# The first stage rebuilt: x normed first, modulation as columns in two halves, projections in pairs, the chunk inverse cut in two

## The chip, the core and the metric

The kernel runs on one core of a Trainium2 chip. The metric is the device time of one execution in microseconds (us). The engines are PE (TensorE, matrix products; PEld is its weight load), DVE (VectorE), ACT (ScalarE), POOL (GpSimd) and SP (SyncE, which here only issues DMAs). SBUF is the working memory, PSUM holds the matrix products.

## What is computed

Two transformer blocks on 512 tokens of width 1024, all in float32. The change lies in the first stage of the first block:

```python
mod = silu(c) @ ada_w + ada_b          # 1024 x 6144
shift1, scale1, gate1, shift2, scale2, gate2 = split(mod, 6)
h = rms_norm(x, norm1_g) * (1 + scale1) + shift1
z = h @ w_in                            # 1024 x 3328
# columns of z: r, k, v (512 each), decay and iclr lora (64 + 64),
# gate lora (128), then q, k, v of the attention (512 each)
```

r, k, v and the lora columns are mixed with the token before (token shift) and feed a recurrence, state = state * w - (state kk)(kk a) + v k, in 8 heads. The kernel computes the recurrence in 8 chunks of 64 tokens, and for each chunk and head it needs the inverse of a 64x64 triangular matrix. The other q, k, v feed a stick-breaking attention with 8 heads. Both results go through w_out; then come a mixture of 32 experts, and a second block with convolution, sparse attention and a feed-forward part.

## The kernel before, in words

`phase_a` (L291) is the first stage. Every large product is three PE products of a high and a low part (`mm3`, L98): a weight tile is cut by `wsplit` (L112) into wh, a cast on ACT (L104), and wl = w - wh, a subtraction on DVE (L105). `wload` (L107) fetches raw weights through SP into `nraw` = 4 buffers of 512 KB.

The order at the start: `params` (L170) fetches small parameters and turns silu(c) into columns; then the 16 loads of `ada_group(0)` (L269) bring shift1 and scale1, each used at once as four one-row PE products (tile adap). x is loaded as one 2 MB transfer held back behind the seventh of these loads (L327). From adap the row tile mod is copied, turned (L332) and split into scale and shift columns (L333, L335). x is normed (L338), turned block by block (L342), and from PSUM written as hH (ACT) and as hL (DVE, L345 and L346).

Then `proj` (L366) takes 128 columns of w_in at a time: 24 products of 512 columns (8 blocks of k times 3), and before each it draws two steps of the remaining modulation, `ada_group(1)` and `(2)`, whose 32 loads feed the same kind of one-row products. First come the two lora chunks, k and r of head pair 0; the lora products follow; then, for each head pair, k, r, v and `prep` (L417), which computes Q1 and Q2 (decayed r, kk, v; and a*kk, k).

`chunk_inverse` (L635) makes XA with 64 small products (tr<-Q,Q), sends its diagonal blocks through DRAM by POOL's DMA queue (xd, XD), runs a recursion of 31 steps with two DVE instructions each (L671, L673), and sends the result back (ed, ET). Its second part turns a block (L681) and joins the two diagonal blocks by 128 products in eight groups, with a DVE copy behind each (L688, L694). The attention's q, k, v projections stand behind it in the program. The chain over chunks and the attention (`sb_heads`, L697) begin when all of this is done.

The order of instructions on each engine is chosen by a scheduler that works from estimated durations, by program order as priority. At run time every engine works its queue in that order.

Of the kernel before, what the change touches and what calls it, by code (L numbers as in the profile page):

```python
# [7 lines left out]
F32 = mybir.dt.float32  # L8
# [4 lines left out]
AF = mybir.ActivationFunctionType  # L13
OP = mybir.AluOpType
# [4 lines left out]
T = 512  # L19
D = 1024  # L20
NT = T // 128
KD = D // 128
CH = 64
NCH = T // CH
# [38 lines left out]
class Ker:  # L63
    def __init__(self, ctx, tc, a, out):
        self.ctx, self.tc, self.nc, self.a, self.out = ctx, tc, tc.nc, a, out
        self.tbl, self.tblusers, self.whl, self.parts = None, [], None, 1
# [103 lines left out]
    def params(self, ps):  # L170
        nc, a, cp = self.nc, self.a, self.cp
        es = ExitStack()
        tp = self.pool(es, "prow", side="right")
        tr = lambda: ps.tile([128, 512], F32, name="tr", tag="tr", bufs=2)
        c8 = tp.tile([8, 128], F32, name="c8")
        nc.scalar.dma_start(c8, a["c"][0].rearrange("(n p) -> n p", p=128))
        self.adab = [(self.hp if g else self.pre).tile([4, 512], F32, name=f"adab{g}") for g in range(3)]
        for g in range(3):
            nc.gpsimd.dma_start(self.adab[g], a["ada_b"][0, g * 2048:(g + 1) * 2048].rearrange("(q c) -> q c", c=512))
        silu = self.act(c8, c8, AF.Silu)  # L180
        p0 = tr()
        nc.tensor.transpose(p0[:, 0:8], c8, self.ident[:8, :8])
        self.ccol = cp.tile([128, 8], F32, name="ccol")
        nc.vector.tensor_copy(self.ccol, p0[:, 0:8])
# [17 lines left out]
        add("norm1_g", rows(a["norm1_g"][0]), 8)  # L202
# [16 lines left out]
        nc.gpsimd.dma_start(pr2[66:88, :], rows(a["ffn_conv_b_2"][0]))  # L219
        n1 = at  # L220
# [48 lines left out]
    def ada_group(self, g, pool, ps):  # L269

        nc, a = self.nc, self.a
        p = ps.tile([128, 512], F32, name="adap", bufs=1)
        self.mm(p, self.sel4, self.adab[g], True, False)
        for k in range(KD):
            for z in range(2):
                w = self.wload(a["ada_w"][0, k * 128:(k + 1) * 128, g * 2048:(g + 1) * 2048]
                               .rearrange("k (q z c) -> k z q c", q=4, z=2)[:, z], [4, 256])
                for q in range(4):
                    self.mm(p[32 * q:32 * q + 1, z * 256:(z + 1) * 256], self.ccol[:, k:k + 1], w[:, q, :], False, k == KD - 1)
                yield  # L280
        m = self.mod[g] = (self.cp if g else pool).tile([128, 512], F32, name=f"mod{g}")
        nc.vector.tensor_copy(m, p)
# [8 lines left out]
    def phase_a(self):  # L291
# [15 lines left out]
        self.sel4 = self.cp.tile([4, 128], F32, name="sel4")  # L307
        nc.vector.tensor_copy(self.sel4.rearrange("p (q r) -> p q r", q=4),
                              self.ident[0:4, 0:4].unsqueeze(2).to_broadcast([4, 4, 32]))
        self.wp = self.pool(RE, "wpa", side="right")  # L310
        self.nraw, self.nhl = 4, 2
# [6 lines left out]
        self.params(psum)  # L318
        self.angles()
        P = lambda tag, bufs: psum.tile([128, 512], F32, name=tag, tag=tag, bufs=bufs)  # L320


        self.mod = {}
        for n, _ in enumerate(self.ada_group(0, pre, psum)):
            if n == 6:
                with tc.issue_after(self.wdma.ins):
                    nc.sync.dma_start(x, a["x"][0].rearrange("(i p) d -> p i d", p=128))  # L327
        m0 = self.mod[0]
        sc = self.cp.tile([128, 16], F32, name="ss1")
        for j in range(4):  # L330
            t = P("tr", 2)
            nc.tensor.transpose(t[:, :128], m0[:, j * 128:(j + 1) * 128], self.ident)  # L332
            nc.vector.tensor_copy(sc[:, j:16:4], t[:, 0:128:32])  # L333

        nc.vector.scalar_tensor_tensor(sc[:, 8:16], sc[:, 8:16], 1.0, self.cols("norm1_g", 8), op0=OP.add, op1=OP.mult)  # L335
        rs = self.rstd_rows(pre, x, D, xn)
        for i in range(NT):
            nc.vector.tensor_scalar(xn[:, i, :], x[:, i, :], rs[:, i:i + 1], None, op0=OP.mult)  # L338
        for k in range(KD):
            t = P("tr", 2)  # L340
            for i in range(NT):
                nc.tensor.transpose(t[:, i * 128:(i + 1) * 128], xn[:, i, k * 128:(k + 1) * 128], self.ident)  # L342
            self.act(hH[:, k, :], t, AF.Identity, bias=sc[:, k:k + 1], scale=sc[:, 8 + k:9 + k])
            hf = pre.tile([128, T], F32, name="hf", bufs=2)
            nc.vector.tensor_scalar(hf, t, sc[:, 8 + k:9 + k], sc[:, k:k + 1], op0=OP.mult, op1=OP.add)  # L345
            nc.vector.tensor_sub(hL[:, k, :], hf, hH[:, k, :].bitcast(F32))  # L346
        es.close()


# [3 lines left out]
        w_in = a["w_in"][0]  # L353
        wnext = {}

        def wchunk(c0, n=128):
            w = self.wload(w_in[:, c0:c0 + n].rearrange("(k p) c -> p k c", p=128), [KD, n])
            return self.wsplit(w)

        def ada_rest():  # L360
            for g in (1, 2):
                yield from self.ada_group(g, hp_, psum)

        ada = ada_rest()

        def proj(wc, c, ncol=128):  # L366
            next(ada, None)
            next(ada, None)
            p = P("mm", 3)
            for k in range(KD):  # L370
                self.mm3(p[:ncol], [t[:, c:c + ncol] for t in wc[k]], (hH[:, k, :], hL[:, k, :]),
                         k == 0, k == KD - 1)
            return p
# [20 lines left out]
        shifted(proj(wchunk(1536), 0), 12, lo)  # L394
        gl = tmp("gl", bufs=1)
        shifted(proj(wchunk(1664), 0), 13, gl)
        kz0, rz0 = tmp("kz"), tmp("rz")
        shifted(proj(wchunk(512), 0), 4, kz0)
        shifted(proj(wchunk(0), 0), 0, rz0)
# [3 lines left out]
        self.act(sgl, gl, AF.Sigmoid)  # L403
        sg = tmp("sg", (128, NT, T), 1)
        for i in range(NT):
            p = P("mm", 3)
            mm(p, th[:, i * 128:(i + 1) * 128], du)
            self.act(sg[:, i, :], p, AF.Sigmoid)
        aT = tmp("aT", (128, 4, T), 1)
        for h in range(4):  # L410
            p = P("mm", 3)
            mm(p, iu[64:128, h * 128:(h + 1) * 128], lo[64:128, :])
            self.act(aT[:, h, :], p, AF.Sigmoid, bias=self.col("iclr_a0", h))
# [3 lines left out]
        def prep(h, k, r):  # L417
            E2 = tmp("E2", (128, NCH, CH + 1), 1)
# [8 lines left out]
            nc.gpsimd.tensor_copy(lam[:, h, :], E2[:, :, CH])  # L427
            sq = tmp("sq", bufs=1)
# [7 lines left out]
            v3 = lambda t: t.rearrange("p (c t) -> p c t", t=CH)  # L436
# [9 lines left out]
            nc.vector.tensor_mul(Q1[:, h, :, 0, :], v3(r), E2[:, :, 1:CH + 1])  # L446

        for h in range(4):
            if h:
                kz, rz = tmp("kz"), tmp("rz")  # L450
                shifted(proj(wchunk(512 + 128 * h), 0), 4 + h, kz)
                shifted(proj(wchunk(128 * h), 0), h, rz)
            else:
                kz, rz = kz0, rz0
            shifted(proj(wchunk(1024 + 128 * h), 0), 8 + h, Q1[:, h, :, 2, :])
            prep(h, kz, rz)
# [15 lines left out]
        kT = lqs.tile([128, 4, T], F32, name="kT")  # L472
        V = lqs.tile([128, NT, T], F32, name="V")
        pp = self.pool(RE, "prep2", side="right")
        self.chunk_inverse(RE, Q1, Q2, ET, P)

        for base, g, dst in ((1792, self.qg8, qT), (2304, self.col("k_norm_g"), kT)):
            for h in range(4):
                headnorm(proj(wchunk(base + 128 * h), 0), g, dst[:, h, :], pp, lambda: P("st", 2))
        for h in range(4):  # L480
            vt = pp.tile([128, T], F32, name="vt", bufs=2)
            nc.scalar.copy(vt, proj(wchunk(2816 + 128 * h), 0))
# [152 lines left out]
    def chunk_inverse(self, RE, Q1, Q2, ET, P):  # L635
# [40 lines left out]
        for b in range(2):  # L676
            s = slice(32 * b, 32 * b + 32)
            nc.gpsimd.dma_start(ET[s, :, s], ed[b].rearrange("u s t -> s u t"))

# [1151 lines left out]
```

## Time and profile before

| what | us |
|---|---|
| median of 3 runs | 2531.09 (2524.82 to 2544.93) |
| the profiled execution | 2528.63 |
| its span, first to last instruction | 2526.8 |
| PE busy in the span | 2432.6 (96%) |
| DVE busy | 1837.4 (73%) |
| ACT busy | 1378.7 (55%) |
| POOL busy | 389.9 (15%) |

Outside the span lie 1.8 us. The busy shares are means over stages with different limits; PE's are pipelined matmuls whose ends are modelled, so that two neighbours overlap. "PEclk" in the rows is the TensorE clock that was granted, as a part of 2.4 GHz: 0.50 is 1.2 GHz.

### The profile page before, as it was taken

The page shows a single profiled execution, that of the slowest core. Times are in us where ns is not written, and L with a number is a line of the kernel's source. Part 1 is how long each engine was busy: PE and PEld are TensorE (multiplying, and loading weights), DVE is VectorE, ACT ScalarE, POOL GpSimd, SP SyncE. Part 2 cuts the span into 40 slices and gives each one's busy share as a digit, 9 for nine tenths or more (in the row PEclk, how much of TensorE's full clock was granted, in tenths as well). Part 3 has the DMA queues.
Part 4 walks back from the last instruction along what each step waited for, and adds up shares of the span by engine and source line. Part 5 has one row for each costly group of instructions (what it writes and reads, how often), then busy time and mean ns, then how long its engine had stood idle before and what let it go on. Part 6 is the DMA issues. An engine that isn't in the chain of part 4 may idle for free. (4 is left out here: it accounts for less than half of the span.)

```text
span 2526.8 us, 33228 instructions
## 1 busy us (share of the span) xinstructions
PE 2432.6 (96%) x12362; PEld 1785.6 (71%) x12362; DVE 1837.4 (73%) x2627; ACT 1378.7 (55%) x1956; POOL 389.9 (15%) x319
## 2 busy tenths in 40 slices
PE   6999998979999999999999999998999999899999
PEld 2677764756777777777777777667877678688887
DVE  3445566689999999999999999986765544555522
ACT  2433455357777777777777777764445543332221
POOL 2000223214221333233210111130100000000000
PEclk7999799989999999999999999998999999899999
DMA  9462100679999999999999999983411131433331
GB/s 277 151 199 67 50 1 30 231 250 337 349 375 370 369 374 375 371 370 369 367 368 366 369 373 372 373 250 103 94 51 42 43 89 63 119 96 99 93 100 67
DMA packets 371566, 556.75 MB, mean 220 GB/s; under 512 B 13138, under 2 KB 153501, under 8 KB 371401
## 3 DMA queue, kind: packets, MB, share of 16 engines
q1 hardware_dynamic: 359808, 518.81, 59.1%
q0 software_dynamic: 11120, 34.68, 6.0%
q8 instruction: 98, 1.61, 0.3%
q10 hardware_dynamic: 473, 1.11, 0.1%
q14 instruction: 67, 0.55, 0.1%
HBM read 534.06 MB, written 20.48 MB: 219 GB/s over the span
## 5 line engine op out<-in xcount | busy, mean ns | idle before, releaser
L105 DVE TENSOR_TENSOR wl<-wraw,wh 128x1024 fp32r<-128x1024 f32 (+2 forms) x974 | 1080.6, 1157 | 253.2 <-ACT wh L104 239.7
L104 ACT CAST wh<-wraw 128x1024 fp32r<-128x1024 f32 (+1 forms) x980 | 942.2, 998 | 542.8 <-PE mm L96 236.4
L96 PE MATMUL hid<-wh,xt 128*96 128x512 f32 x2048 | 671.4, 396 | 0.6 <-DVE xt L1066 0.5
L96 PEld LDWEIGHTS hid<-wh,xt 128*96 128x96 f32 x2048 | 331.5, 162 | 138.0 <-DVE xt L1066 1.2
L96 PE MATMUL hid<-wl,xt 128*96 128x512 f32 x1024 | 402.0, 393 | 0.0
L96 PE MATMUL y<-wh,at 128*96 128x512 f32 x960 | 310.0, 393 | 0.0
L1225 POOL DMA_INDIRECT acc<-ys,tli x30 | 190.6, 6353 | 545.1 <-DVE ys L1134 525.5
L96 PE MATMUL mm<-hH,wh 128*128 128x512 f32 x624 | 253.4, 407 | 3.3 <-ACT gate L1600 1.9
L96 PE MATMUL mm<-hL,wh 128*128 128x512 f32 x624 | 248.9, 399 | 0.0
L96 PE MATMUL mm<-hH,wl 128*128 128x512 f32 x624 | 248.7, 399 | 0.0
L96 PEld LDWEIGHTS hid<-wl,xt 128*96 128x96 f32 x1024 | 166.1, 162 | 63.9 <-issue 0.3
L96 PEld LDWEIGHTS y<-wh,at 128*96 128x96 f32 x960 | 155.4, 162 | 66.8
L96 PE MATMUL y<-wl,at 128*96 128x512 f32 x480 | 188.4, 393 | 0.0
L96 PEld LDWEIGHTS mm<-hH,wh 128*128 128x128 f32 x624 | 118.6, 190 | 37.3 <-issue 5.7
L96 PEld LDWEIGHTS mm<-hL,wh 128*128 128x128 f32 x624 | 118.4, 190 | 28.2 <-issue 3.8
L96 PEld LDWEIGHTS mm<-hH,wl 128*128 128x128 f32 x624 | 118.5, 190 | 27.1 <-issue 2.6
L74 ACT ACTIVATE gl<-gl 96x512 f32<-96x512 f32 x64 | 40.5, 632 | 156.9 <-DVE gl L1073 156.9
L96 PEld LDWEIGHTS y<-wl,at 128*96 128x96 f32 x480 | 77.6, 162 | 32.8
L1052 POOL DMA_INDIRECT xg<-h2d,tli x32 | 45.8, 1431 | 292.9 <-PE tr L1060 285.6
L96 PE MATMUL mu<-hH,wh 128*128 128x512 f32 x176 | 68.5, 389 | 0.0
L96 PE MATMUL mu<-hL,wh 128*128 128x512 f32 x176 | 68.5, 389 | 0.0
L96 PE MATMUL mu<-hH,wl 128*128 128x512 f32 x176 | 68.5, 389 | 0.0
(558 smaller groups left out, 3361.8 us busy)
## 6 DMA issues: line engine op xcount, KB each, us to landing
wraw<-in_exp_w_dram SPq DMA_DIRECT2D x384, 1024.0 KB
wraw<-in_w_in_dram SPq DMA_DIRECT2D x62, 512.0 KB
wraw<-in_ada_w_dram SPq DMA_DIRECT2D x48, 512.0 KB
wraw<-in_w_ffn_in_dram SPq DMA_DIRECT2D x44, 512.0 KB
wraw<-in_w_ffn_out_dram SPq DMA_DIRECT2D x22, 512.0 KB
wraw<-in_w_out_dram SPq DMA_DIRECT2D x4, 1024.0 KB
wraw<-in_w_o_dram SPq DMA_DIRECT2D x8, 512.0 KB
acc<-zf SPq DMA_DIRECT2D x1, 2432.0 KB
```

The source lines that it names most:

```text
L74: ins = self.nc.scalar.activation(out, in_, func, **kw)
L96: self.nc.tensor.matmul(out, l, r, start=start, stop=stop, skip_group_check=True)
L104: self.nc.scalar.copy(h, src)
L105: (eng or self.nc.vector).tensor_sub(l, src, h.bitcast(F32))
L1052: self.gathered = nc.gpsimd.indirect_dma_start(out=xg, out_offset=None, in_=self.h2d, in_offset=bass.IndirectOffsetOnAxis(ap=self.tli[:, e ...
L1225: self.nc.gpsimd.indirect_dma_start(out=self.acc, out_offset=bass.IndirectOffsetOnAxis(ap=idx, axis=0), in_=ys, in_offset=None, compute_op ...
```

## The change

- x comes first on SP, in four transfers; it is normed and turned to xT before the modulation is there. hH and hL are then made from xT in SBUF.
- shift1 and scale1 are made in two halves A and B of 512 columns, 8 loads each. Of every half, some loads are multiplied by their column of silu(c) and summed in a tile by ACT and DVE (`mul`, `add`), some go through PE with the weights as the stationary side (`dot`); a last `dot` with ones gives columns at once, so that no row has to be turned.
- The first four chunks of w_in (lora, gate, two of k) are multiplied half by half. All of this runs in an order written by hand for PE, ACT, DVE and SP.
- gate1 and the second block of modulation (32 loads): ACT multiplies each in place, POOL adds it to a sum, and two PE products per 1024 columns finish it, instead of the products of each load.
- w_in is then taken in `pairs` of two chunks, in two loads of 512 rows by 256 columns. `nraw` is 5, `nhl` 3.
- All k come first, `prep` for four head pairs follows, then the first part of the inverse, then r, v, q, k; the second part of the inverse stands behind k and before the attention's v.
- prep copies the decay into Q1 on POOL; r multiplies it in place later (`rho`). The angles of the second block move behind the hand-ordered part.

```diff
-        self.nraw, self.nhl = 4, 2
+        self.nraw, self.nhl = 5, 3
...
-    def ada_group(self, g, pool, ps):
...
-                for q in range(4):
-                    self.mm(p[32 * q:32 * q + 1, z * 256:(z + 1) * 256], self.ccol[:, k:k + 1], w[:, q, :], False, k == KD - 1)
+    def ada_rest(self, pool, P):
...
+                for k in range(KD):
+                    w = self.wload(a["ada_w"][0, k * 128:(k + 1) * 128, c0:c0 + D], [D])
+                    self.act(w if k else acc, w, AF.Copy, scale=self.ccol[:, k:k + 1])
+                    if k:
+                        nc.gpsimd.tensor_add(acc, acc, w)
+                    yield
+                p = P("st", 2)
+                for q in range(2):
+                    r = slice(64 * z + 32 * q, 64 * z + 32 * q + 1)
+                    self.mm(p[r], self.ones[:, 0:1], acc[:, 512 * q:512 * q + 512])
+                    nc.vector.tensor_add(self.mod[g][r], p[r], self.mod[g][r])
...
+            def dot(h, w, col):
+                for j in range(8):
+                    self.mm(h.p[:, j:j + 1], w[:, 128 * j:128 * j + 128], col, not h.begun, False)
+                    h.begun = True
+            def mul(h, k, w):
+                self.act(h.acc, w, AF.Copy, scale=self.ccol[:, k:k + 1])
+            def add(h, k, w):
+                nc.vector.scalar_tensor_tensor(h.acc, w, self.ccol[:, k:k + 1], h.acc, op0=OP.mult, op1=OP.add)
...
+        with tc.manual_schedule(engines={ET_.PE, ET_.Activation, ET_.DVE, ET_.SP}):
+            for i in range(NT):
+                nc.sync.dma_start(x[:, i, :], a["x"][0, 128 * i:128 * i + 128])
...
+            wa = [A.load(k) for k in range(3)]
...
+            A.mul(0, wa[0])
+            A.dot(wa[1], self.ccol[:, 1:2])
+            A.add(2, wa[2])
+            w = A.load(3)
+            A.dot(w, self.ccol[:, 3:4])
+            for k in range(KD):
...
+                nc.scalar.copy(xT[:, k, :], t)
+            for k in range(4, KD):
+                A.add(k, A.load(k))
+            raw = [wpart(c0, 0) for c0 in (1536, 512)]
+            wb = [B.load(k) for k in range(3)]
+            heads = [P4() for _ in range(4)]
+            w0 = self.wsplit(raw[0])
+            A.columns()
+            hT(0)
+            hT(1)
+            w1 = self.wsplit(raw[1])
+            hT(2)
+            hT(3)
+            for k in range(4):
+                for c in range(2):
+                    part(heads[c], w0, 128 * c, 0, (k,))
+            B.mul(0, wb[0])
+            B.add(1, wb[1])
+            B.dot(wb[2], self.ccol[:, 2:3])
+            for k in (3, 4):
+                B.add(k, B.load(k))
+            part(heads[2], w1, 0, 0)
+            B.dot(B.load(5), self.ccol[:, 5:6])
+            for k in (6, 7):
+                B.add(k, B.load(k))
+            raw = [wpart(c0, 1) for c0 in (1536, 512)]
+            w0 = self.wsplit(raw[0])
+            B.columns()
+            part(heads[3], w1, 128, 0)
...
+        def pairs(c0, use):
+            for _ in range(3):
+                next(ada, None)
+            w = []
+            for h in range(2):
+                w += self.wsplit(wpart(c0, h))
+            for c in range(2):
+                p = P4()
+                for h in range(2):
+                    part(p, w[4 * h:4 * h + 4], 128 * c, h)
+                use(c, p)
...
+        pairs(768, lambda c, p: shifted(p, 6 + c, kz[2 + c]))
...
+            nc.gpsimd.tensor_copy(Q1[:, h, :, 0, :], E2[:, :, 1:CH + 1])
...
+            prep(h, kz[h])
...
+        inverse = self.chunk_inverse(RE, Q1, Q2, ET, P)
+        next(inverse)
+        def rho(h, p):
+            rz = tmp("hnq", (128, T), 1)
+            shifted(p, h, rz)
+            nc.vector.tensor_mul(Q1[:, h, :, 0, :], v3(rz), Q1[:, h, :, 0, :])
+        for j in range(2):
+            pairs(256 * j, lambda c, p: rho(2 * j + c, p))
+        for j in range(2):
+            pairs(1024 + 256 * j, lambda c, p: shifted(p, 8 + 2 * j + c, Q1[:, 2 * j + c, :, 2, :]))
+        for base, g, dst in ((1792, self.qg8, qT), (2304, self.col("k_norm_g"), kT)):
+            for j in range(2):
+                pairs(base + 256 * j, lambda c, p: headnorm(p, g, dst[:, 2 * j + c, :], pp, lambda: P("st", 2)))
+        next(inverse, None)
...
+        for j in range(2):
+            pairs(2816 + 256 * j, lambda c, p: values(2 * j + c, p))
```

## Rows read from the trace of the kernel before

**Rows 1.** Stretches: length, busy of five engines (count), PEclk, DMA share, GB/s.
```profile
0.00:26.00 26.00, 8.24 (x59) 1.98 (x59) 2.39 (x19) 2.87 (x3) 13.28 (x61) 0.79 0.86 266
...
41.20:54.00 12.80, 11.52 (x63) 5.80 (x64) 7.66 (x14) 5.09 (x6) 0.00 (x0) 0.68 1.02 307
54.00:252.40 198.40, 196.92 (x1074) 139.04 (x1072) 101.40 (x165) 76.72 (x107) 9.75 (x29) 1.00 0.49 141
252.40:269.20 16.80, 13.58 (x257) 13.54 (x256) 7.65 (x9) 0.00 (x0) 0.00 (x0) 0.55 0.53 178
269.20:282.00 12.80, 12.76 (x55) 9.71 (x54) 7.13 (x20) 8.96 (x27) 5.33 (x12) 0.52 0.06 12
300.00:420.00 120.00, 119.14 (x888) 79.41 (x886) 71.45 (x144) 71.90 (x164) 34.05 (x59) 1.00 0.00 1
```

**Rows 2.** Timeline: SP's load of x, PE's first and steady products.
```profile
12.31 0.53 SPq L327 DMA_DIRECT2D Q<-in_x_dram  x1
...
49.59 0.74 PE L96 MATMUL mm<-hH,wh 128*128 128x512 f32 x2
...
104.10 0.39 PE L96 MATMUL mm<-hL,wh 128*128 128x512 f32 x1
104.33 0.39 PE L96 MATMUL mm<-hH,wl 128*128 128x512 f32 x1
```

**Rows 3.** Stretches of the start and of 20 to 30 us, columns as in rows 1.
```profile
1.00:2.00 1.00, 0.00 (x0) 0.00 (x0) 0.92 (x8) 0.07 (x1) 0.87 (x5) 1.00 0.12 26
...
20.00:30.00 10.00, 2.31 (x17) 0.39 (x17) 0.55 (x4) 3.96 (x7) 0.00 (x0) 0.50 1.06 345
```

**Rows 4.** Timeline: a 128x1024 three-operand DVE instruction, eight weight loads, one hH.
```profile
505.47 1.28 DVE L892 SCALAR_TENSOR_TENSOR h2r<-x,rsy,g 128x1024 f32<-128x1024 f32 x1
...
46.95 1.57 PEld L342 LDWEIGHTS tr<-ident,Q 128*128 128x128 f32 x8 [0.86 <-issue]
...
48.11 1.63 ACT L74 ACTIVATE hH<-tr,ss 128x512 fp32r<-128x512 f32 x2 [0.28 <-PE tr L342]
```

**Rows 5.** Groups of PE, 54 to 252.4 us: count, busy us, mean ns.
```profile
L96 PE MATMUL mm<-hH,wh 128*128 128x512 f32 x204 | 82.8, 407 | 0.0
...
L96 PE MATMUL adap<-wraw,ccol 128*1 128x256 f32 x224 | 17.7, 378 | 0.8 <-DMA wraw<-in_ada_w_dram 0.8
L96 PE MATMUL st<-sq,bones 128*128 128x512 f32 x8 | 4.1, 593 | 0.0
L342 PE MATMUL tr<-ident,Q 128*128 128x128 f32 x16 | 2.3, 279 | 0.0
```

**Rows 6.** Timeline between the last projection and the chain.
```profile
251.75 0.66 PE L485 MATMUL st<-ident,vt 128*128 128x128 f32 x4 [0.73 <-ACT vt L482]
253.27 2.30 DVE L681 STREAM_TRANSPOSE XA<-ET 32x2048 f32<-32x2048 f32 x1 [2.45 <-DMA ET<-ed]
...
269.23 0.80 PE L96 MATMUL sl<-qT,kT 64*128 64x128 f32 x4
```

**Rows 7.** Groups of DVE and ACT, 54 to 252.4 us, columns as in rows 5.
```profile
L105 DVE TENSOR_TENSOR wl<-wraw,wh 128x1024 fp32r<-128x1024 f32 x24 | 29.4, 1223 | 48.1 <-ACT wh L104 39.6 <-PE st L96 8.5
L673 DVE TENSOR_TENSOR E<-E,Et 128x31 f32<-128x31 f32 (+15 forms) x31 | 10.6, 341 | 0.9
L671 DVE TENSOR_TENSOR Et<-E,XD 128x31 f32<-128x31 f32 (+15 forms) x31 | 10.6, 341 | 3.3 <-DMA XD<-xd 2.4
...
L104 ACT CAST wh<-wraw 128x1024 fp32r<-128x1024 f32 x24 | 25.1, 1047 | 72.5 <-PE mm L96 64.0 <-DMA wraw<-in_w_in_dram 8.0 <-ACT sgl L74 0.5
```

**Rows 8.** Timeline of POOL and DVE, 485 to 496 us: start, us.
```profile
484.95 10.30 POOL L105 TENSOR_TENSOR wl<-wraw,wh 128x1024 fp32r<-128x1024 f32 x4 [1.78 <-ACT wh L104]
...
490.81 1.72 DVE L853 SCALAR_TENSOR_TENSOR rowi<-pos,ef 128x4 int32<-128x4 f32 x1
...
493.04 2.24 DVE L859 TENSOR_TENSOR pos<-tf,pos 128x4 f32<-128x4 f32 x1
...
499.95 0.16 DVE L859 TENSOR_TENSOR pos<-tf,pos 128x4 f32<-128x4 f32 x1
```

More of the change, by code (lines that the diff above doesn't have):

```diff
@@ L317, in phase_a @@
         pre = self.pre = self.pool(es, "pre", side="right")
-        self.params(psum)
-        self.angles()
[L320 to L346, printed above, removed]
@@ L347, in phase_a, with part @@
-        es.close()
+        P = lambda tag, bufs: psum.tile([128, 512], F32, name=tag, tag=tag, bufs=bufs)
+        P4 = lambda: P("mm", 4)
+        w_in = a["w_in"][0]
+        wpart = lambda c0, h: self.wload(w_in[512 * h:512 * h + 512, c0:c0 + 256].rearrange("(k p) c -> p k c", p=128), [4, 256])
+        sc = self.cp.tile([128, 16], F32, name="ss1")
+        def part(p, w, c, h, ks=range(4)):
+            for k in ks:
+                kk = 4 * h + k
+                self.mm3(p, [t[:, c:c + 128] for t in w[k]], (hH[:, kk, :], hL[:, kk, :]), kk == 0, kk == KD - 1)
@@ new lines, in phase_a, with __init__, load, columns @@
+        class Half:
+            def __init__(h, b):
+                h.b, h.begun = b, False
+                h.p, h.acc = P("st", 2), pre.tile([128, D], F32, name="acc0", bufs=2)
+            def load(h, k):
+                w = self.wload(a["ada_w"][0, k * 128:(k + 1) * 128, 0:2048]
+                               .rearrange("k (z h c) -> k z h c", z=2, h=2)[:, :, h.b], [2, 512])
+                return w.rearrange("p z c -> p (z c)")
+            def dot(h, w, col):
[6 more added lines that the diff above has]
+                nc.vector.scalar_tensor_tensor(h.acc, w, self.ccol[:, k:k + 1], h.acc, op0=OP.mult, op1=OP.add)
+            def columns(h):
+                b, p, v = h.b, h.p, sc[:, 8 + 4 * h.b:12 + 4 * h.b]
+                h.dot(h.acc, self.ones[:, 0:1])
+                nc.vector.tensor_add(sc[:, 4 * b:4 * b + 4], p[:, 0:4], self.ccol[:, 16 + 4 * b:20 + 4 * b])
+                nc.vector.scalar_tensor_tensor(v, p[:, 4:8], 1.0, self.ccol[:, 24 + 4 * b:28 + 4 * b], op0=OP.add, op1=OP.add)
+                nc.vector.tensor_mul(v, v, self.ccol[:, 8 + 4 * b:12 + 4 * b])
@@ L350, in phase_a @@
+        es.close()
+        self.angles()
+        ada = self.ada_rest(hp_, P)
+        def pairs(c0, use):
[4 more added lines that the diff above has]
+                w += self.wsplit(wpart(c0, h))
+            for c in range(2):
+                p = P4()
+                for h in range(2):
+                    part(p, w[4 * h:4 * h + 4], 128 * c, h)
+                use(c, p)
         PP = ExitStack()
@@ L352, in phase_a @@
         tmp = lambda name, shape=(128, T), bufs=2: pp.tile(list(shape), F32, name=name, tag=name, bufs=bufs)
[L353 to L373, printed above, removed]
         def shifted(p, m, dst):
@@ L393, in phase_a @@
         lo = tmp("lo", bufs=1)
[L394 to L399, printed above, removed]
+        shifted(heads[0], 12, lo)
+        shifted(heads[1], 13, sgl)
+        kz = [tmp("kz", bufs=4) for _ in range(4)]
+        for h in range(2):
+            shifted(heads[2 + h], 4 + h, kz[h])
+        pairs(768, lambda c, p: shifted(p, 6 + c, kz[2 + c]))
         th = tmp("th", (65, T), 1)
@@ L472, in phase_a, with values @@
         kT = lqs.tile([128, 4, T], F32, name="kT")
-        V = lqs.tile([128, NT, T], F32, name="V")
[L474 to L482, printed above, removed]
+        pp = self.pool(RE, "prep2", side="right")
+        tmp = lambda name, shape, bufs=2: pp.tile(list(shape), F32, name=name, tag=name, bufs=bufs)
+        inverse = self.chunk_inverse(RE, Q1, Q2, ET, P)
[12 more added lines that the diff above has]
+        next(inverse, None)
+        lqs = self.pool(LQ, "lqv", side="left")
+        V = lqs.tile([128, NT, T], F32, name="V")
+        def values(h, p):
+            vt = tmp("sh", (128, T + 1))[:, 0:T]
+            nc.scalar.copy(vt, p)
             p = P("st", 2)
```

93 lines of the change are left out of this document (57 added, 36 removed).

## The prediction

> **What bounds the kernel now.** I read the stretches first, because the busy shares of the whole span mix stages with different limits. From 54 to 252.4 us PE is busy 196.92 of 198.40 us at full clock, with DMA at half its share and ACT and DVE half idle: this stretch lasts as long as PE's list of work. Before 54 us it is otherwise: from 0 to 26 us PE is busy 8.24 us of 26, and up to 54 us its mean clock is low (0.68 in the last 12.8 us) [rows 1]. The 8 MB of the first modulation group and x come through DMA, which saturates at some 345 GB/s [rows 3]; x itself is only issued at 12.31 us, and the first product with hH starts at 49.59 us [rows 2]. Then the timeline shows a second hole. The last turning of v ends at 252.4 us, DVE turns ET at 253.27 us, and the attention starts at 269.23 us [rows 6]; in between PE does only the 256 small product records of the inverse's second part, 13.58 us at a clock of 0.55, and the 12.8 us behind it still run at 0.52 [rows 1]. From then on PE is busy again (119.14 of 120 us, [rows 1]), and the later stages start when the one before has ended. So whatever is won before the chain should reach the end whole; I found no wait on something outside this order.
>
> **Change 1, the start.** x (2.10 MB), the eight loads of half A (4.19 MB) and two w_in parts (1.05 MB) are 7.34 MB. DMA moves little before 2 us [rows 3]; with 345 GB/s from 2.3 us on, the last load of A lands at 2.3 + 6.29/0.345 = 20.5 us, the w_in parts at 23.6 us. Five buffers don't hold this up as long as a load is used up within some 4 us, since squares and norming are done while A comes in. Behind A's last load stand one DVE add (1.28 us, [rows 4]), sixteen weight loads of `dot` at half clock (eight took 1.57 us, so 3.1 us, [rows 4]), three short DVE instructions (some 0.8 us with handovers, an estimate) and one hH (0.8 us, [rows 4]): products start at about 26.5 us, 23 us sooner than before. Half B's loads could land by 23.6 + 8 x 1.52 = 36 us, but B's last load takes the buffer of its third, which PE frees only behind the first 24 products. These take 24 x 0.456 = 11 us at half clock, from 26.5 us to 37.5 us; with the dot (3 us at half clock, less at full) the buffer is free at about 39 us, and the load lands at 41 to 43 us. Add, dot, columns and hH cost 5 us again: 47 us. Of the 96 products of four chunks, 48 are then left, minus nothing that the wait could still take: 11 us at full clock. So four chunks are done at **57 us**, with 54 us if B7 is not held up, and 69 us if all 48 run at half clock (47 + 22).
>
> **Change 2, PE's list behind it.** A 512-column product takes 0.2277 us from start to start (104.10 to 104.33 us, [rows 2]). The stretch from 54 to 252.4 us holds 616 of them in three like groups, of which the first is shown [rows 5]: 140.3 us; in the changed kernel 528 of 624 are left at 57 us: 120.2 us. Gone are the one-row products of the modulation (17.7 us, and 1 to 2 us of the row with the bias) and the last turnings of x (2.3 us, [rows 5]). The rest of PE's list, 198.4 - 140.3 - 17.7 - 1.5 - 2.3 = 36.6 us, stays. Added are eight products of ones with the sums: four of that size take 4.1 us [rows 5], so 4 us if the two of a pair run beside each other in different columns, 8 us if not; I take 5. The second part of the inverse, 13.6 us at half clock, comes into this list, beside the attention's v, at full clock: 6.8 us. Sum: 120.2 + 36.6 + 5 + 6.8 = 168.6 us. 57 + 168.6 + 1.5 (copying and turning the last v) = 227 us, against 269.2 us: **42 us less**, if nothing stalls PE.
>
> For the inverse to be hidden its first part must be done when the last k is projected. Its recursion is 62 DVE instructions, 21.2 us in all [rows 7], and it now has r, v, q and k, 16 chunks of 24 products (5.5 us each, 87 us), in front of the second part, where before 12 chunks stood beside it. Even twice as long it is in time, and the two v pairs are 22 us more of cover. POOL's DMA hops stand behind its adds now; four hops late by one add each are 10 us, which this cover takes.
>
> **Change 3, the clock at the chain's start.** Where PE comes from full work, I expect the 12.8 us at 0.52 [rows 1] to run at full clock. At most half of it goes, 6 us; none goes if ACT, busy 8.96 us there, or the handovers set the pace. I take 3.
>
> **At nothing.** The product of r with the decay stays one DVE instruction of the same size, only later; the four copies of the decay on POOL (some 1.3 us each, half of a subtraction, [rows 8]) are hidden while prep waits for DVE anyway, and cost up to 5 us if they hold up an add that frees a buffer. The angles' DVE work goes from the DMA-bound start to the stretch of the first projections, some 6 us on an engine that is half idle there; without this cover it would delay the first wl behind the heads by as much. The scheduler orders everything anew; I have no row for what that does to later stages.
>
> **Change 4, the sums on ScalarE and GpSimd.** ACT's 32 scalings cost like a cast of that size, 1.05 us [rows 7]: 33 us on an engine that is busy 76.72 us of 198.4 [rows 1]. Hidden, though its queue gets fuller. POOL gets 28 adds of 128x1024; four subtractions of that size took 10.30 us [rows 8], 2.58 us each: 72 us on an idle engine. This is not free for DVE. Rows 8 show DVE instructions with two SBUF operands that stand still while POOL runs: L853, a few numbers, takes 1.72 us and L859 2.24 us until a POOL subtraction ends, while the same L859 with POOL idle takes 0.16 us. DVE's busy time of 101.4 us [rows 1] and POOL's 72 us together, minus some 6 us of DVE work that goes, make 167 us if the two never overlap: just the length of PE's list. On the mean it fits; where DVE is dense it doesn't. Beside the recursion, 33 us of PE work, stand 21.2 us of it, six cuts wl (7.3 us, [rows 7]) and three pairs with up to 9 adds, less those at k = 0: 8, 21 us. That is 50 us of work that excludes each other, 17 us more than PE has there; the third wh and wl buffer gives back half a pair, some 3 us. I charge **14 us** of PE waiting for wl. Bounds: 0 if the scheduler's order spreads it, 42 us if each of 28 adds costs PE 1.5 us.
>
> The Trainium skill has the rule on "SBUF — State Buffer", section "Who interferes with whom": a DVE instruction with two SBUF inputs and a GpSimd instruction that reads SBUF exclude each other, and the later one waits for the whole of the other. The rows of 485 to 496 us agree (0.16 us became 2.24 us). By this rule a copy from PSUM isn't hit, so that a part of DVE's list does run beside POOL; without the rule the sum would be 14 us lower.
>
> **The sum.** -42 - 3 + 14 = -31 us. Against the profiled 2528.63 us this gives **2498 us**; the median of the runs lies 2.5 us above that execution, so that the same gain from there would read 2500 us.
>
> **The rivals.** (a) POOL's adds are hidden: the adds come at 3 per 11 us of PE and fall where DVE has slack. For it: DVE idles 97 of 198.4 us before [rows 1]. Against it: the recursion was dense and now has both. The time is 2528.6 - 45 = 2484 us. (b) DVE's queue is worse: PE waits 1.2 us per add, 34 us, because prep of four head pairs, cuts and adds now come together as well. 2528.6 - 45 + 34 = 2518 us. (c) The start doesn't do what it says: B waits for its buffer and both halves of the products run at half clock. Four chunks are done at 69 us; with 14 us of waits, 2510 us. Speaks for it: PE's clock was 0.50 all through the stretch of sparse work [rows 3]. (d) Slower: each add holds up the cut of the next weights for its full 2.58 us, because DVE's order is fixed from durations that know nothing of POOL, and PE has no product left meanwhile. 28 x 2.58 = 72 us: 2528.6 - 45 + 72 = 2556 us. It decides from the point where PE waits over 45/28 = 1.6 us per add. Against it: the wh and wl of half a pair are there ahead, and many adds fall on ACT's or DMA's delays.
>
> **How the numbers follow.** Forecast 0.46 (its own range 2488 to 2508 us), (a) 0.24, (b) 0.14, (c) 0.09, (d) 0.07. A measurement of this kernel can tell about 1%, 25 us, from no change. Faster by over that (below 2503 us) are all of (a), three quarters of the forecast and a little of (c): 0.61. Slower by over 1% is half of (d): 0.03. The rest, 0.36, lies between. The range takes in (a) with a start at 54 us (2480 us) and (b) with a few us more (2522 us).
>
> **What would show each step.** In the changed trace: the first product mm<-hH at 24 to 30 us, not 49.6; four chunks done at 54 to 60 us; no tile adap; wraw of ada_w read by ACT and by POOL, 28 POOL adds of 2.5 us; DVE wl or the recursion's instructions drawn out to 2 us or more where POOL is busy, and PE idle "<-DVE wl" in sum 8 to 20 us; the inverse's small products among products mm with v, at full clock; the attention's first sl at 230 to 250 us, and all later stages earlier by the same. I am wrong if sl starts at the right time but the end doesn't move (then something behind the chain has slack), if the PE waits lie before 57 us (then change 1 is mis-sized), or if PE's idle time names ACT or DMA and not DVE (then change 4's mechanism is another).

## The result and the profile after

The changed kernel takes 2579.81 us (median of 4 runs, 2565.66 to 2581.26) against 2538.01 us (4 runs beside them): ratio 1.0147, 95% interval 1.011 to 1.0183. It is slower by about 1.5%, where 2498 us was forecast. The profiled execution took 2581.26 us, its span 2579.4 us.

Two rows of PE's timeline of the changed kernel, the first product with hH and the first of the attention:

```profile
31.11 0.79 PE L96 MATMUL mm<-hH,wh 128*128 128x512 f32 x1 [2.06 <-ACT hH L74]
...
281.99 0.49 PE L96 MATMUL sl<-qT,kT 64*128 64x128 f32 x4
```

The start does come sooner (31.1 against 49.6 us, [rows 2]), yet the attention starts 12.8 us later than before (269.2 us, [rows 6]). The stretches of the changed kernel that answer to [rows 1], all with their length, the busy time and count of PE, PEld, DVE, ACT and POOL, the granted clock, DMA's share and GB/s; the cuts are the first product, the end of the first four chunks, the first sl, the last sl and the first expert product:

```profile
0.00:26.00 26.00, 13.62 (x59) 11.86 (x60) 13.21 (x39) 13.11 (x21) 13.45 (x30) 1.00 0.80 283
31.00:72.00 41.00, 37.04 (x146) 29.69 (x146) 29.78 (x37) 17.77 (x21) 15.98 (x40) 0.77 0.70 220
72.00:282.00 210.00, 184.84 (x1018) 134.79 (x1018) 132.84 (x180) 96.25 (x129) 74.06 (x67) 0.91 0.43 137
282.00:457.00 175.00, 169.78 (x1061) 110.06 (x1061) 94.58 (x188) 92.11 (x210) 42.16 (x75) 0.86 0.01 1
457.00:573.00 116.00, 85.10 (x400) 63.68 (x398) 74.52 (x163) 39.82 (x75) 26.32 (x25) 0.83 0.54 188
```

In the third row PE stands still for 25 us of 210 and its mean clock is 0.91; before, it was busy 196.92 of 198.40 us at 1.00 [rows 1]. POOL is busy 74 us there. The fourth row, the chain, was 153.3 us long before and is 175 us, at a mean clock of 0.86.

Later the kernel before was profiled once more (2543.6 us, close to its median). That execution is the better one to compare with, as the chain will show. Lengths of the stages in us, cut at the same instructions:

| stage | before | before again | after | after again |
|---|---|---|---|---|
| to the first sl | 269.2 | 269.3 | 282.0 | 284.6 |
| first to last sl (chain) | 153.3 | 165.5 | 175.0 | 175.0 |
| to the first expert product | 108.7 | 110.4 | 116.1 | 115.9 |
| from there to the end | 1995.5 | 1996.6 | 2006.4 | 2008.4 |
| span | 2526.8 | 2541.8 | 2579.4 | 2583.8 |

Against "before again", the first profile after loses 12.7, 9.5, 5.7 and 9.7 us: 37.6 us in four places, of which I had foreseen none as a loss.

### The profile page after: what moved, and what is told of

The parts are those of the page before. It is cut to its first block, busy times and chain, and to the rows that moved or that the text cites. A ratio compares the mean times of both kernels' runs of the same rounds, so it can differ in the third digit from the quotient of the medians.

```text
span 2579.4 us, 32819 instructions
## 1 busy us (share of the span) xinstructions
PE 2464.0 (96%) x12080; PEld 1810.1 (70%) x12080; DVE 1892.0 (73%) x2648; ACT 1424.7 (55%) x1998; POOL 520.8 (20%) x359
## 5 line engine op out<-in xcount | busy, mean ns | idle before, releaser
L1326 POOL DMA_INDIRECT acc<-ys,tli x30 | 246.4, 8214 | 504.0 <-DVE ys L1235 503.7
L96 PE MATMUL mm<-hH,wh 128*128 128x512 f32 x624 | 259.3, 416 | 14.0 <-DVE lo L472 5.8
L96 PE MATMUL mm<-hL,wh 128*128 128x512 f32 x624 | 257.3, 413 | 3.5 <-DVE hL L374 3.5
L96 PE MATMUL mm<-hH,wl 128*128 128x512 f32 x624 | 255.7, 410 | 2.3 <-DVE wl L105 2.3
L287 POOL TENSOR_TENSOR acc<-acc,wraw 128x1024 f32<-128x1024 f32 x28 | 70.5, 2516 | 103.2 <-ACT wraw L74 90.0
## 6 DMA issues: line engine op xcount, KB each, us to landing
wraw<-in_exp_w_dram SPq DMA_DIRECT2D x384, 1024.0 KB, 10.7
```

The costliest lines, as they stand in the source:

```text
L96: self.nc.tensor.matmul(out, l, r, start=start, stop=stop, skip_group_check=True)
L287: nc.gpsimd.tensor_add(acc, acc, w)
L1326: self.nc.gpsimd.indirect_dma_start(out=self.acc, out_offset=bass.IndirectOffsetOnAxis(ap=idx, axis=0), in_=ys, in_offset=None, compute_op ...
```

## The experiments

**GpSimd's adds.** What PE waited for between its first product and the first sl in the changed kernel (in total, times, longest, us):

```profile
PE mm L96 <- DVE lo L472: 5.8, 1, 5.8
PE st L96 <- DVE mod L293: 4.8, 1, 4.8
PE mm L96 <- DVE hL L374: 3.5, 2, 2.7
PE tr L96 <- DVE Q L532: 3.5, 1, 3.5
PE mm L96 <- ACT sg L74: 3.0, 1, 3.0
PE mm L96 <- DVE qT L550: 2.9, 2, 1.9
PE mm L96 <- DVE wl L105: 2.3, 2, 2.0
```

Most name DVE, but six different tiles of it, and of these six wl is the least. That the adds also hold the buffers of the raw weights (SP waits 70.7 us for them) is not what holds PE: no wait above names a load, and from 72 us on the casts wh wait for PE alone. The timeline of POOL and DVE shows the cause:

```profile
52.06 2.38 POOL L287 TENSOR_TENSOR acc<-acc,wraw 128x1024 f32<-128x1024 f32 x1 [36.17 <-ACT wraw L74]
52.65 2.35 DVE L374 TENSOR_TENSOR hL<-hf,hH 128x512 fp32r<-128x512 f32 x1 [2.51 <-ACT hH L74]
...
54.92 0.54 DVE L373 TENSOR_SCALAR hf<-Q,ss 128x512 f32<-128x512 f32 x1
...
55.56 0.69 DVE L374 TENSOR_TENSOR hL<-hf,hH 128x512 fp32r<-128x512 f32 x1
...
56.87 2.75 POOL L287 TENSOR_TENSOR acc<-acc,wraw 128x1024 f32<-128x1024 f32 x1 [2.42 <-ACT wraw L74]
57.30 2.60 DVE L373 TENSOR_SCALAR hf<-Q,ss 128x512 f32<-128x512 f32 x1
...
65.39 5.94 POOL L287 TENSOR_TENSOR acc<-acc,wraw 128x1024 f32<-128x1024 f32 x2
65.98 0.24 DVE L231 COPY pcol<-tr 128x80 f32<-128x80 f32 x1 [2.90 <-PE tr L230]
...
69.00 2.35 DVE L1416 CAST pf<-pi 128x4 f32<-128x4 int32 x1
```

The same hL takes 0.69 us alone and 2.35 us beside an add, the same hf 0.54 and 2.60 us: DVE gets on only when the add is nearly over. `e_noadd` takes the adds away; the modulation rows then hold other values, so that only the time up to the end of the chain is read.

```diff
                     self.act(w if k else acc, w, AF.Copy, scale=self.ccol[:, k:k + 1])
-                    if k:
-                        nc.gpsimd.tensor_add(acc, acc, w)
```

> The changed kernel without the 28 adds on GpSimd: the last two modulation groups then hold only the last scaled slices, so that what comes behind the attention has other values and only phase A and the chain are read. Theory (GpSimd's adds hold up DVE and the queues that wait for them, and the waits bring PE's clock down): the first sl comes at 250 to 262 us instead of 282, DVE's one-input instructions hf, hL, wl stay near their short times (hL 0.6 us and not 2.4), and the half-clock stretches between 57 and 282 us, 44 us in the changed kernel, shrink to under 25. Rival (ACT's scalings, the PSUM buffers and the order of the loads hold PE): sl at 275 to 282 us, waits on lo and hH as before.

The first sl came at 256.5 us, 25.5 us sooner, and hL took its short time of 0.69 us again (the expectation calls hL and wl one-input; both have two). Half-clock stretches between 57 us and the first sl fell from 44.3 to 13.6 us. DVE's groups from 75 to 250 us, first of the changed kernel (count, busy us, mean ns, idle before):

```profile
L105 DVE TENSOR_TENSOR wl<-wraw,wh 128x1024 fp32r<-128x1024 f32 x19 | 31.0, 1643 | 12.4 <-ACT wh L104 12.3
L564 DVE TENSOR_TENSOR Q<-hnq,Q 128x512 f32<-128x512 f32 x4 | 5.5, 1369 | 0.1
```

and the same two without the adds:

```profile
L105 DVE TENSOR_TENSOR wl<-wraw,wh 128x1024 fp32r<-128x1024 f32 x19 | 23.2, 1221 | 12.5 <-ACT wh L104 12.4
L562 DVE TENSOR_TENSOR Q<-hnq,Q 128x512 f32<-128x512 f32 x4 | 2.8, 692 | 0.1
```

The stretch of `e_noadd` behind the first four chunks, columns as above:

```profile
68.00:256.50 188.50, 175.36 (x1018) 129.11 (x1018) 102.02 (x171) 95.72 (x129) 15.55 (x38) 0.96 0.47 148
```

This stretch holds 171 instructions of DVE and that of the changed kernel 180. From the start to the first sl both kernels have the same 259, first the changed kernel's, then those of `e_noadd`:

```profile
0.00:282.00 282.00, 238.43 (x1244) 178.77 (x1245) 178.95 (x259) 130.24 (x173) 103.49 (x136) 0.90 0.52 166
...
0.00:256.45 256.45, 225.42 (x1243) 170.80 (x1244) 142.22 (x259) 129.53 (x173) 32.72 (x108) 0.95 0.57 183
```

DVE's busy time falls from 178.95 to 142.22 us with nothing taken off DVE: 37 us of it had been standing still. So the theory holds. Its size is less sure: without the adds the scheduler also orders anew (at most 240 of DVE's 259 instructions keep their order), and the 25.5 us hold both. Of the rival a part is true, since the wait on lo grew here:

```profile
PE mm L96 <- DVE lo L470: 10.7, 1, 10.7
```

The chain behind it took 177.6 us in `e_noadd`, 71.7 us of it at half clock, so that 2.6 us of the gain were lost again there.

`e_dve` gives the sums to DVE, multiply and add in one instruction:

```diff
-                    self.act(w if k else acc, w, AF.Copy, scale=self.ccol[:, k:k + 1])
                     if k:
-                        nc.gpsimd.tensor_add(acc, acc, w)
+                        nc.vector.scalar_tensor_tensor(acc, w, self.ccol[:, k:k + 1], acc, op0=OP.mult, op1=OP.add)
+                    else:
+                        self.act(acc, w, AF.Copy, scale=self.ccol[:, k:k + 1])
```

> The changed kernel with the sums of the last two modulation groups on DVE (multiply and add in one instruction, 28 of some 1.3 us, 36 us), no GpSimd adds and only four ACT scalings of these groups. Theory (GpSimd's adds and the fuller ACT queue cost PE the waits): first sl at 255 to 268 us, the time 12 to 25 us below the changed kernel. Rival (DVE is the bound as soon as it has more work): sl at 282 us or later, time the same or above.

First sl at 266.8 us, time 2552.77 us (10 runs), 27 us below the changed kernel and still 1.0039 times before (1.0008 to 1.0069). So 36 us of real work on DVE costs less than POOL's 70.5 us (28 adds of 2.5 us) beside it. The gain is slightly above what was expected, because the chain, too, was 10 us shorter (30.7 us of it at half clock, 47.8 us in the changed kernel).

**The angles, and the parameters.** Two of the named waits were tried by themselves. `e_angles` moves the angles, whose sines stand on ACT ahead of the first heads' shifts:

```diff
         es.close()
-        self.angles()
...
         PP.close()
+        self.angles()
+        self.table("natural_log_exp_and_others")
```

> The changed kernel with the angles' work moved from behind the start to behind the prep of the heads, GpSimd's adds left in. Theory (in the changed kernel the first heads' PSUM buffers come free late because ScalarE does the angles' sines, and DVE their 20 small instructions, ahead of the heads' shifts): the wait of 5.8 us on lo falls below 3 us and the first sl comes 3 to 8 us sooner, at 274 to 280 us. Rival (the shifts are late because of the modulation's scalings and the weight cuts): the wait stays above 4 us, sl within 3 us of 282 to 285.

The wait on lo left the list altogether, as the theory said, and yet the first sl came at 287.6 us: hL 5.1, qT 4.9, wl 4.7 and XA 4.0 us stood there instead. The wait taken away at one place came back at others. The adds are not the whole reason, since `e_combo` (below) shows the same without them. The time was 2581.21 us.

`e_params` moves the parameter loads off ACT's queue. In the changed kernel's timeline the last of them is issued at 11.34 us and the first square follows (the releaser named there, a load of weights, isn't its own input):

```profile
11.34 0.30 ACTq L224 DMA_DIRECT2D pr<-in_ffn_conv_w_dram  x1
...
11.68 1.06 ACT L74 ACTIVATE Q<-Q 128x1024 f32<-128x1024 f32 x1 [8.29 <-DMA wraw<-in_ada_w_dram]
```

```diff
-        eng = [nc.scalar, nc.gpsimd]
+        eng = [nc.gpsimd, nc.gpsimd]
...
-        nc.scalar.dma_start(pr2[0:66, :], ...)
+        nc.gpsimd.dma_start(pr2[0:66, :], ...)
```

> The changed kernel with all parameter loads issued by GpSimd and none but c and the gain by ScalarE, whose first squares stood behind these issues until 11.7 us. Theory (the start is late because of ScalarE's queue): the first square at 7 to 9 us, the first product with hH at 26.5 to 28.5 us instead of 31.1. Rival (the loads of half A, or DVE's list, set the start): the squares come sooner, the first product stays within 1.5 us of 31.1. Behind the start nothing is expected to change by more than that.

The squares did come sooner,

```profile
5.07 1.06 ACT L74 ACTIVATE Q<-Q 128x1024 f32<-128x1024 f32 x1 [1.72 <-DMA Q<-in_x_dram]
```

by 6.6 us, but the first product only by 1.6 us, to 29.5 us: neither side's number. ACT's queue was a small part of the late start; first sl 285.1 us, 2582.43 us. What holds the start in this run is seen in its rows of DVE:

```profile
21.55 2.61 DVE L360 SCALAR_TENSOR_TENSOR acc<-wraw,ccol,acc 128x1024 f32<-128x1024 f32 x2 [2.16 <-DMA wraw<-in_ada_w_dram]
...
26.96 1.23 DVE L105 TENSOR_TENSOR wl<-wraw,wh 128x1024 fp32r<-128x1024 f32 x1 [2.81 <-ACT wh L104]
```

Half A's last add ends at 24.2 us, behind a late load, where the forecast has 21.8 us, and a weight cut stands in front of the scale columns, which the forecast's sum leaves out.

**The pace of the products.** In the second convolution stage PE is busy without a gap in both kernels, and yet slower. PE's products in 100 us (busy time, count in brackets, clock, DMA share, GB/s), first of the changed kernel, then of the kernel before:

```profile
2240.00:2340.00 100.00, 100.00 (x431) 1.00 0.32 95
...
2240.00:2340.00 100.00, 100.00 (x443) 1.00 0.32 95
```

From start to start that is 226.7 ns in the kernel before against 233.3 (the mean over the 86 to 88 pairs of records in each 20 us). A part of the change that I had passed over moves data: the constants' tiles shrank by 448 bytes (sel4 and columns of pcol gone, ccol wider), and with them every tile on the left side of SBUF moved, while the right side stayed. `e_pad` adds the 448 bytes to an unused tile that is there already:

```diff
-        cp.tile([128, 24], F32, name="pad")
+        cp.tile([128, 136], F32, name="pad")
```

> The changed kernel with 448 bytes more of padding among the constants, so that all tiles on the left side of SBUF stand at the addresses that they had before. Theory (the pace of the products hangs on how the addresses of weights and moving operand stand to each other, and the change shifted only one of them): products of the second convolution stage from start to start 226.7 ns instead of 233.3, those of the experts 231.4 instead of 234.3, the time about 11 us below the changed kernel's 2580 us; phase A and the chain as in the changed kernel (first sl at 282 us). Rival (the slower pace belongs to the chip's state or to what runs beside): pitch stays at 233, time 2575 to 2582 us.

```profile
2240.00:2340.00 100.00, 100.00 (x443) 1.00 0.34 98
```

443 products in 100 us, 226.7 ns; first sl at 284.2 us; from the first expert product to the end 1991.1 us against 2006.4; the time 2565.54 us (4 runs), 14 us below the changed kernel. One of the changed kernel's own four runs took 2565.66 us, so the time alone would not decide. The stage does: from the first expert product on, six profiles with the changed constants took 2006.4 to 2011.1 us and the three with the 448 bytes 1988.4 to 1991.1 us. The opposite test, on the kernel before (24 to 40 columns, 64 bytes):

> The kernel before with 64 bytes more of padding, which moves the left-side tiles to another remainder by 128 and nothing else. Theory of the addresses: the pitch of the second convolution stage goes from 226.7 to about 233 ns, the experts' from 231.4 to about 234, the time 8 to 12 us above the kernel before. Rival (remainder by 128 is not what counts, or the pace is not of the addresses): no change, within 3 us.

It became slower: 1.007 times (1.0036 to 1.0105), 7 us by the medians, 233.3 ns, 2012.8 us behind the first expert product. That the addresses set the pace is so shown from both sides. Which remainder counts took two more (56 and 88 columns, 128 and 256 bytes):

> The kernel before with 128 bytes more of padding: every left-side tile moves by 128 bytes, its remainder by 128 stays. Theory (the remainder counts, not that tiles move): pitch of the second convolution stage 226.7 ns, experts 228 to 231, from the first expert product to the end 1994 to 1998 us. Rival (any shift does it, or the remainder by 256 or more): 233 ns and 2008 us or more, as with 64 bytes.

```profile
2240.00:2340.00 100.00, 100.00 (x432) 1.00 0.33 95
```

> The kernel before with 256 bytes more of padding. Remainder by 128 has fallen as the rule: 128 bytes more gave 232.4 ns. In the kernel before, the weights' tiles wh and the moving operand hH2 differ by a multiple of 256 bytes (and not by one of 512). Theory (products are quick when the two addresses are equal by 256): pitch of the second convolution stage 226.7 ns again, from the first expert product to the end 1994 to 1998 us. Rival (only the exact old distance is quick, or a rule by 512 or more): 232 to 234 ns and 2006 us or more.

```profile
2240.00:2340.00 100.00, 100.00 (x443) 1.00 0.33 97
```

With 128 bytes the stage ran at 232.4 ns and my rule by 128 fell; with 256 bytes it ran at 226.7 ns. From the first expert product to the end they took 2006.6 and 1991.4 us, one run each. By the addresses of the built programs, the tiles of the second convolution stage stand so:

| kernel | wh, remainder by 256 | hH2, by 256 | pitch, ns |
|---|---|---|---|
| before; + 256 bytes; after + 448 | 224 | 224 | 226.7 |
| before + 64; after | 32 | 224 | 233.3 |
| before + 128 | 96 | 224 | 232.4 |

So stationary wh and moving hH2 ran quickly where they were equal by 256. The experts do not follow this simply. There wh and wl move and xt and at stay, both at 224. Between neighbouring products at full clock (distances over 240 ns left out) hid takes 230.1 ns with wh at 224, 229.1 at 96 and 233.3 at 32, and y 230.2, 227.0 and 233.4 ns: only the distance of 64 is slow there, and 128 is rather the quickest. In the last products ro<-wh,aH both tiles lie on the left and move together: 227.0 ns before, after and with 128 bytes. Why the distance counts isn't shown.

**The chain.** PE's stretches around the half-clock part of the changed kernel's chain (PE's busy time, count, clock):

```profile
288.00:313.00 25.00, 24.97 (x85) 0.52 0.00 1
313.00:374.00 61.00, 59.96 (x468) 1.00 0.00 1
374.00:398.00 24.00, 24.00 (x108) 0.50 0.00 1
```

TensorE is granted 1.2 GHz twice for 24 us, the second time after 61 us in which it was busy 59.96 us at 2.4 GHz. Both kernels were run once more unchanged, to see whether this repeats.

> The changed kernel itself once more, to see what repeats. Theory (the half-clock stretches inside the chain, 288.8 + 23.9 us and 374.1 + 23.9 us in its first profile, come from the program): stretches of 20 us or more at the same two places, within 10 us, and the last sl 170 to 178 us behind the first. Rival (they fall differently from execution to execution, and the first profile had more than its share): they lie elsewhere or are fewer, and the chain is 13 us shorter for each one that is missing; the spread of 2566 to 2581 us between the runs would be one stretch more or less. The start (first product at 31.1 us, first sl at 282 us within 3 us) and the pitch (233 ns) repeat in either case.

> The kernel before itself once more. If the program sets the half-clock stretches: chain from first to last sl in 153 us within 4 us and no half-clock stretch of over 5 us between 300 and 430 us, as in its first profile. If they fall by chance: a stretch of some 20 us there, the chain longer by 10 us or more, and a time in the upper half of its 2520 to 2559 us.

The changed kernel repeats it, 4 us later with its later start:

```profile
292.00:317.00 25.00, 25.00 (x99) 0.52 0.00 1
317.00:378.00 61.00, 59.97 (x461) 1.00 0.00 1
378.00:402.00 24.00, 24.00 (x105) 0.50 0.00 1
```

The kernel before does not repeat its full clock of 300 to 420 us [rows 1]. The second profile of it, same columns:

```profile
272.00:388.00 116.00, 114.04 (x861) 0.97 0.01 2
388.00:419.00 31.00, 31.00 (x121) 0.51 0.00 1
419.00:434.70 15.70, 15.01 (x69) 0.99 0.00 0
```

So both theories hold for one kernel each. With the order of the kernel before, two of five profiles have no such stretch (before, 64 bytes) and three have one of 30.7 to 44.4 us from 388 us on. With the changed kernel's order all four (after, again, `e_params`, `e_pad`) have two, which begin at nearly the same places of PE's list: at product 29 to 43 and at product 585 to 595 of the chain's 1059 (the second lasts 13.7 us in `e_params` and `e_pad`). The profile from which I forecast was one without: 12 of the 22 us by which the chain grew are this chance. Of the other 9.5 us the clock is a part only. The chain has 15.6 us at half clock in the first profile of the kernel before, 40.8 us in the second and 47.8 us in the changed kernel; 7 us more of it lose 3.5 us. PE also stands still for 5.2 us instead of 2.7, and some 3.5 us stay open. The products are the same 1059, but the scheduler put them into another order: at most 870 stand in the order of before. What makes the chip lower the clock there, with PE busy by its records, stays open.

The 5.7 us behind the chain come from the new order, too. PE waits 5.3 us there on ACT's copy of the gate's row (g). In the changed kernel this copy stands behind a pair of casts that waited for their weights, in the kernel before (second pair of rows) in front of it:

```profile
483.14 1.99 ACT L104 CAST wh<-wraw 128x1024 fp32r<-128x1024 f32 x2 [4.64 <-DMA wraw<-in_w_out_dram]
485.04 0.58 ACT L299 COPY g<-o 128x512 f32<-128x512 f32 x1
...
442.47 0.58 ACT L288 COPY g<-o 128x512 f32<-128x512 f32 x1
446.72 1.99 ACT L104 CAST wh<-wraw 128x1024 fp32r<-128x1024 f32 x2 [3.19 <-DMA wraw<-in_w_out_dram]
```

In `e_dve`, where it stands in front again, the way from the last sl to the first expert product took 110.8 us.

**Repairs together.** `e_dve_pad` is `e_dve` with the 448 bytes.

> The sums on DVE (run e_dve) and the padding (run e_pad) in one kernel. If the two costs are independent: first sl at 267 us within 3 us as with the sums on DVE alone, pitch 226.7 ns, the stretch from the first expert product to the end 1991 to 1997 us as with the padding alone, so a time some 15 us below the 2553 us of e_dve: 2534 to 2541 us, within 0.3% of the kernel before. Rival (the later stages only shift their waits): 2546 us or more.

2532.27 us (12 runs), 0.9983 times before (0.9953 to 1.0012): the two costs add up, with the first sl, the last stage and the time each a little below the range expected. By stages it is 263.0, 165.3, 112.2 and 1988.4 us, so 19.0, 9.7, 3.9 and 17.9 us less than the first profile after; some 50 us together, and the loss of the change is gone. `e_combo` adds to it the parameters on GpSimd, the later angles, and the first four heads' shifts put ahead:

```diff
+        with tc.high_priority():
+            shifted(heads[0], 12, lo)
+            shifted(heads[1], 13, sgl)
+            for h in range(2):
+                shifted(heads[2 + h], 4 + h, kz[h])
```

> Four repairs together: the padding that restores the addresses, the sums of the modulation groups on DVE without GpSimd's adds, parameter loads issued by GpSimd, and the angles moved behind the prep of the heads with the first four heads' shifts put ahead in the order. Theory (each of these is a cost of its own): first product at 27 to 28 us, no wait on lo over 4 us, first sl at 245 to 256 us, pitch 226.7 ns, time 2515 to 2530 us, faster than the kernel before (2540 us). Rival (the chain gives it back at half clock, or the gains overlap): first sl at 255 to 265 us and a time within 8 us of the kernel before.

2546.39 us (12 runs), 1.0029 times before (0.9998 to 1.006). The first product came at 28.8 us and the first sl at 261.6 us, hardly sooner than without these edits, because waits on hH (7.0 us) and on the r's shift (6.2 us) took the place of that on lo. The way from the last sl to the first expert product rose to 117.9 us. The rival was right. No version was found that is measurably faster than the kernel before.

## Why the prediction was wrong

**Change 1** forecast the first product at 26.5 us and four chunks at 57 us (bounds 54 and 69). They came at 31.1 and 72 us, outside the bounds (68.8 and 70.0 us in two more profiles of this order). Of the 4.6 us at the first product ACT's late squares explain 1.6 us (`e_params`); the rest are the late load of half A and the weight cut that the sum leaves out. The 96 products took 41 us at a mean clock of 0.77, some 19 us of them at half clock, as rival (c) had it in part. I had also let POOL's adds begin to cost only behind the start; without them four chunks were done at 65.7 us, as the drawn-out hL and hf (52 to 60 us) belong to half B.

**Change 2's list** holds for PE's work, but its condition "if nothing stalls PE" failed: with the adds away, PE needs 190.8 us from four chunks (65.7 us) to the first sl, 20.7 us more than the 170.1 us worked out. From 68 us on it stands still for 13.1 us of these, 10.7 of them on lo, and 13.6 us at half clock lose 6.8 us more. The wait on lo is a term that I had put at nothing, the angles, on "an engine that is half idle there": it is 5.8 us in the changed kernel and goes when the angles go (`e_angles`). The second part of the chunk inverse is hidden, as forecast: PE waits 0.7 us on XA.

**Change 4** failed by its size, and in its place. The mechanism was right: an add excludes DVE's instructions with two SBUF operands (hL 0.69 and 2.35 us). The Trainium skill's "SBUF — State Buffer", section "Who interferes with whom", names tensor_scalar, copy and cast as well where they run in a mode with both ports. I had left these out. hf (0.54 to 2.60 us) and the small cast pf (2.35 us) agree with it, though no row shows in which mode they ran; pcol's copy from PSUM, 0.24 us beside an add, agrees, too. The charge of 14 us became 25.5 us, a new order included. It was worked out for the recursion alone; for the rest I added busy times over the whole stretch (101 and 72 us in 167), though DVE's work also stands on chains (shift, prep, cut) in which a standstill is passed on to PE. Beside the recursion (187 to 233 us) PE's longer waits make only 6.9 us; 17.1 us of them lie between 72 and 148 us, on lo, sg, mod and prep's Q. And I counted PE's waits alone: its clock was at half for 44.3 us between 57 and 282 us, 13.6 us without the adds, and half of such time is lost on top. The test I gave for it, 8 to 20 us of "<-DVE wl", was wrong in the name: 2.3 us. So the first sl, forecast at 227 + 14 = 241 us, is late by three terms: 8.7 us of the start without adds (65.7 for 57), 20.7 us of the list, and 25.5 - 14 = 11.5 us of the adds, together the 41 us up to 282.

**Change 3** took 3 us for a full clock at the chain's start. The clock there was 1.2 GHz for 24 us from 288.8 us on.

**"Whatever is won before the chain should reach the end whole"** was the second failure, and no rival had it. The chain took 22 us more by the first profiles, of which the clock makes some 16 us, and 9.5 us by the second of before, of which it makes 3.5 us. "The scheduler orders everything anew" stood at nothing, without a row; it cost the 5.7 us behind the chain and perhaps the rest of the chain's. The addresses took another 10 to 15 us, a cost that the prediction has nowhere: I read the diff for instructions and not for the sizes of tiles, so that a gap of 448 bytes among the constants had no term.

**The base.** The profiled execution of 2528.63 us lay 11 us below the median of the 19 runs made later (2539.64), not 2.5 us; its chain had none of the half-clock stretch that is 12 us in "before again".

Rival (d), the slower one, gave 2556 us from 2.58 us per add; its sign was right, its mechanism only in part: per add PE lost 25.5/28 = 0.9 us, less than the 1.6 us from which it decides. The rest of the loss lay where no rival looked, so that (d) is no nearer to the cause for having the sign.

## What to carry to other kernels

An add on an idle GpSimd isn't free for DVE: here 70 us of it held DVE up for 37 us and the first stage for some 25 us, and the same sums as fused instructions on DVE were cheaper. A change in one stage can reorder the ones behind it: compare their order, too. When a change adds or drops even a small constant, compare the tiles' addresses before and after; 64 bytes were worth 0.7% of this kernel. And take a second profile of the kernel before: a stretch that looks steady in one execution (the clock of the chain) may be a matter of that execution.

## What was not expected of the hardware

- The pitch of 512-column products hangs on the addresses of their operands: 226.7 ns where wh and hH2 agree by 256 bytes, 232.4 to 233.3 ns at distances of 128 and 64, over hundreds of microseconds of full clock. In the experts only the distance of 64 is slow.
- PE's clock was lowered to 1.2 GHz while PE was busy (59.96 of 61 us before it fell), at nearly the same products (585 to 595 of 1059) in four profiles of one order, and only in some profiles of another.
- A DVE instruction with one tensor operand in SBUF and two columns as scalars (hf) stood still beside a GpSimd add, too: 0.54 us became 2.60 us.
